# Sums over features and heads: constant-matrix products in float32r halves, and late gates' tanh at another place

## The chip, the cores and the metric

The kernel runs on one core of a Trainium2 chip. A core has a matrix engine (TensorE; PE in the profile, with PEld for its weight loads), VectorE (DVE), ScalarE (ACT), GpSimd (POOL) and a queue engine that issues most of the DMAs (SyncE; SP). Each engine works through its own list of instructions in order and waits for the others by semaphores. The metric is the device time of one execution in microseconds (us); lower is better.

## The reference

One layer of a hybrid block on x of 512 frames by 1024 features, all in float32. What matters here, shortened:

```python
def rms_norm(x, g):
    return x * lax.rsqrt(jnp.mean(x * x, axis=-1, keepdims=True) + 1e-6) * g

x = x + 0.5 * swiglu(rms_norm(x, ffn1_norm), w1, w3, w2)        # d_ff = 2816
p = rms_norm(x, mix_norm) @ W_in
# rwkv7_mixer on token-shifted columns of p, 8 heads of 64:
kk = kk / maximum(sqrt(sum(kk * kk)), 1e-12)                    # per head
y = rwkv7_recurrence(r, decay, k, v, -kk, kk * a)               # state per head, frame by frame
mu = mean(y); var = mean(square(y - mu))                        # per head
y = (y - mu) * rsqrt(var + eps) * lnx_g + lnx_b
bonus = sum(r * k * r_k) * v                                    # per head
y_a = ((y + bonus) * (sigmoid(g_lo) @ g_up)) @ rwkv_proj
y_b = forgetting_attention(rms_norm(q), rms_norm(k), v, log_f) @ fox_proj
x = x + (sigmoid(g_A) * y_a + sigmoid(g_B) * y_b) @ w_out
x = x + 0.5 * swiglu(rms_norm(x, ffn2_norm), w1, w3, w2)
out = rms_norm(x, final_norm)
```

## The kernel before, in words

Activations lie transposed: features on the 128 partitions, the 512 frames along the free dimension. x is 8 tiles of 128x512 (`xT`). A large product is made of float32r products of 128x128 weights by 128x512 activations. float32r is a float32 with a shortened mantissa, so every operand is split in two halves: `hi`, a cast to float32r (ScalarE, `act.copy`), and `lo`, the rest (VectorE, a subtraction). `mm3` (L122 to L125) then makes three products: whi by xhi, whi by xlo, wlo by xhi. A float32r product of this size shows as one record, a full float32 one as two.

Weights come as blocks of up to 8x128x128: `load_raw` (DMA, three buffers `raw`), then `split_w` (cast at L115 into one of two buffers `whi`, subtraction at L116 into one of two `wlo`). A cast into `whi` must wait until the products that read that buffer's previous content are through.

The stages, with their place in the profiled execution:

1. 0 to 26 us: x is loaded and transposed, the first gate and up column of the first FFN is made as the tiles arrive (`f0`, `f1`). `Norm.square` takes squares of the 8 tiles and adds seven of them in `acc` (GpSimd or VectorE); the eighth stays in `last`.
2. To 380 us: first FFN, 22 column pairs (`pa`, `pb`), then 8 output blocks (`pd`). `Norm.finish` (L192) sums the squares over partitions with a product by the matrix `ones`, once for `acc` (L194) and once for `last` (L195), in full float32; then ln (`rln`) and exp (`rstd`, L199) on ScalarE. The gate reads `rstd` at L329 (`fa`) and so empties the bank of `pa`.
3. 380 to 406: mixer's norm finish, the low-rank codes (`pl`, `pz`) with their sigmoids (L455).
4. 406 to 520: four steps `step(p)`, one per head pair: columns k, r, v and a gate, small products per chunk (`gp`), the key norm's head sum, and the bonus: `rk` = r k r_k, summed per head by a full float32 product with `bones`, the block matrix of ones (L589), then times v and stored.
5. 540 to 726: the delta rule as a scan over 16 chunks of 32 frames, with the attention and its columns filling between; each chunk writes its part of `V4` (the four tiles `vs`).
6. 726 to 784, the late stage: `fox_proj` (`ppj<-yh`), interleaved with the head norm of the rule: `yc` = `center` by y (L881, full float32, `center` is identity less mean), its square, the variance sum with `bones` (L885, full float32), ln, exp, scale and shift, the output gate product (L893), and the split in `ya`. Then `rwkv_proj` (`ppj<-ya`). The merge gates of the first seven columns get their tanh at L918, all behind `roots`, the last head pair's exp, since another table set has to be loaded on ScalarE for tanh.
7. To 830 `w_out` (`pw`), then second FFN and final norm to 1207.

The order on each engine is set when the kernel is built: a scheduler with its own estimate of durations lists the instructions of each engine by data dependences, free buffers and a few marks (`tc.issue_after(x)`: not before x in the list; `tc.keep_in_program_order`). On the chip each list runs strictly in order. PSUM banks come from three pools: `pm` (2 banks), `pr` (3) and `pf` (3).

The attention's q and k norms sum their squares already by two float32r products with `bonesr`, through the helper `headsum` (cast L136, subtraction L139, products L140 and L141).

Of the kernel before, what the change touches and what calls it, by code (L numbers as in the profile page):

```python
# [9 lines left out]
F32 = mybir.dt.float32  # L10
F32R = mybir.dt.float32r
BF16 = mybir.dt.bfloat16
AF = mybir.ActivationFunctionType
ALU = mybir.AluOpType
# [4 lines left out]
P = 128  # L19
T = 512  # L20
# [5 lines left out]
NP = DA // P  # L26
# [24 lines left out]
def kernel(  # L51
# [7 lines left out]
    dve, act, pool, pe = nc.vector, nc.scalar, nc.gpsimd, nc.tensor  # L59

    cp = ctx.enter_context(tc.tile_pool(name="cp", bufs=1))
# [8 lines left out]
    def bank(name, pool_=None):  # L70
        pool_ = pool_ or pm
        return pool_.tile([P, T], F32, tag="b", name=name)

    def tmp(name, shape=(P, T), dt=F32, tag="t", **kw):
        return tp.tile(list(shape), dt, tag=tag, name=name, **kw)
# [5 lines left out]
    dve.tensor_copy(identb[:], ident[:])  # L81
    ones = cp.tile([P, P], F32, name="ones")
    dve.memset(ones[:], 1.0)
    bones = cp.tile([P, P], F32, name="bones")
    dve.memset(bones[:], 0.0)
    dve.memset(bones[0:64, 0:64], 1.0)
    dve.memset(bones[64:128, 64:128], 1.0)
    center = cp.tile([P, P], F32, name="center")
    dve.scalar_tensor_tensor(center[:], bones[:], -1.0 / 64, ident[:], op0=ALU.mult, op1=ALU.add)
    bonesr = cp.tile([P, P], F32R, name="bonesr")  # L90
    dve.tensor_copy(bonesr[:], bones[:])
# [37 lines left out]
        tc.keep_in_program_order(pre)  # L129
        tc.keep_in_program_order(act.activation(out, in_, AF.Ln, **kw))  # L130

    def headsum(ps, src, hi=None, lo=None, eng=None):
        hi = tmp("shi", dt=F32R)[:] if hi is None else hi
        lo = tmp("slo", dt=F32R)[:] if lo is None else lo
        if eng is act:
            act.copy(hi, src)  # L136
        else:
            dve.tensor_copy(hi, src)
        dve.tensor_tensor(lo, src, hi.bitcast(F32), op=ALU.subtract)  # L139
        pe.matmul(ps, bonesr[:], hi, start=True, stop=False)  # L140
        pe.matmul(ps, bonesr[:], lo, start=False, stop=True)  # L141

    def split(dst_hi, dst_lo, src, hi_eng="act"):
        if hi_eng == "act":
            act.copy(dst_hi, src)
        else:
            dve.tensor_copy(dst_hi, src)
        dve.tensor_tensor(dst_lo, src, dst_hi.bitcast(F32), op=ALU.subtract)


    xctx = ExitStack()
# [3 lines left out]
    class Norm:  # L155
# [35 lines left out]

        def finish(s):  # L192
            ps = bank("ssum", pr)
            pe.matmul(ps[:], ones[:], s.acc[:], start=True, stop=False)  # L194
            pe.matmul(ps[:], ones[:], s.last[:], start=False, stop=True)  # L195
            ln = tmp("rln")
            ln_act(ln[:], ps[:], bias=epsr[:, 0:1], scale=1.0 / D)
            s.rstd = xp.tile([P, T], F32, tag="rstd", name="rstd")
            act.activation(s.rstd[:], ln[:], AF.Exp, scale=-0.5)  # L199
# [10 lines left out]
    def pc(i):  # L210
        return par[:, i:i + 1]
# [11 lines left out]
    with tc.tile_pool(name="x0", bufs=1) as x0:  # L223
# [7 lines left out]
        for c in range(KD):  # L231
            ps = bank("xtp", pr)
# [149 lines left out]
    with ExitStack() as mx:  # L382
        rp = mx.enter_context(tc.tile_pool(name="rp", bufs=1))
# [6 lines left out]
        def duo(tag, name, dt=F32):  # L390
            return sp.tile([P, 2, T], dt, name=name, tag=tag)
# [30 lines left out]
        la = rp.tile([P, T], F32, name="la", tag="la")  # L422
# [27 lines left out]
        for p in range(NP):  # L450
            za.append((zslots[2 * p], zslots[2 * p + 1]))
            for i, (w_, x_, par0, o) in enumerate(((uw, lw, PAR_W0, zslots[2 * p]), (ux, lx, PAR_A0, zslots[2 * p + 1]))):
                ps = bank("pz", (pr, pf)[i])
# [7 lines left out]
        t2 = pctx.enter_context(tc.tile_pool(name="t2", bufs=1, side="right"))  # L461
# [8 lines left out]
        vs = [V4[:, p] for p in range(NP)]  # L470
# [10 lines left out]
        def work(name, dt=F32):  # L481
            late = name in ("kka", "rk", "bon")
            return t2.tile([P, T], dt, name=name, tag="sb" if late else "sa", bufs=3 if late else 5)
# [23 lines left out]
        def step(p):  # L507
# [10 lines left out]
            sq = work("ksq")  # L518
            act.activation(sq[:], kk[:], AF.Square)
            hi, lo = work("khi", F32R), work("klo", F32R)  # L520
# [15 lines left out]
            ps = bank("pn", pf)  # L536
# [3 lines left out]
            rn = work("krn")  # L540
# [8 lines left out]
            for q in range(2):  # L549
                s = slice(q * 64, (q + 1) * 64)  # L550
                dve.scalar_tensor_tensor(G[p][q][s, :, 0, :], ch(kk)[s], -1.0, Pp[s, :, 0:C],
                                         op0=ALU.mult, op1=ALU.mult)
            for q in range(2):
                s = slice(q * 64, (q + 1) * 64)
# [6 lines left out]
            for a_ in range(2):  # L561
                with tc.issue_after(mms[5].ins):
                    for c in range(8):
                        for q in range(2):
                            g = (a_ + q) % 2
                            s = slice(q * 64, (q + 1) * 64)
# [3 lines left out]
                for q in range(2):  # L570
                    g = (a_ + q) % 2
# [5 lines left out]
                        op=ALU.mult)  # L577
# [7 lines left out]
            rk = work("rk")  # L585
            dve.scalar_tensor_tensor(rk[:], r[:], pc(PAR_RK + p), k[:], op0=ALU.mult, op1=ALU.mult)
            ps = bank("pn", pr)
            with tc.issue_after(gm.ins):
                pe.matmul(ps[:], bones[:], rk[:], start=True, stop=True)  # L589
            bon = work("bon")  # L590
            dve.tensor_tensor(bon[:], ps[:], v[:], op=ALU.mult)
            act.activation(bon[:], bon[:], AF.Identity, bias=pc(PAR_LB + p))
# [7 lines left out]
        t2 = fctx.enter_context(tc.tile_pool(name="fx", bufs=1, side="right"))  # L600
# [8 lines left out]
        for t in range(C - 1):  # L609
            n, m = t + 1, C - 1 - t  # L610
# [47 lines left out]
        def norm_qk(p):  # L658
            if p < NP // 2:
                for o, par0 in qks[p]:  # L660
                    dve.tensor_tensor(o[:], o[:], mix.rstd[:], op=ALU.mult)
            sums = []
            for o, par0 in qks[p]:
                sq = tmp("qsq")
                act.activation(sq[:], o[:], AF.Square)
                ps = bank("pq2", pf)
                headsum(ps[:], sq[:], eng=act)
                sums.append(ps)
            for (o, par0), ps in zip(qks[p], sums):
                rn = tmp("qrn")  # L670
                act.activation(rn[:], ps[:], AF.Ln, bias=epsr[:, 0:1], scale=1.0 / 64)
                qks["last"] = act.activation(rn[:], rn[:], AF.Exp, scale=-0.5)
                dve.scalar_tensor_tensor(o[:], o[:], pc(par0), rn[:], op0=ALU.mult, op1=ALU.mult)
            qks[p] = [o for o, par0 in qks[p]]
# [95 lines left out]
        dve.scalar_tensor_tensor(nf[FR, :], fz[FR, :], 0.0, nf[FR, :], op0=ALU.min, op1=ALU.subtract)  # L770
        dve.tensor_tensor_scan(fz[FR, :], ones[FR, 0:1].broadcast_to([8, T]), nf[FR, :], initial=0.0, op0=ALU.mult, op1=ALU.subtract)

        klc = [t2.tile([P, T], F32R, name=f"klc{q}") for q in range(2)]
        for q in range(2):
            o = (1 - q) * 64
            pool.memset(f32(klc[q][:]), 0.0)
# [7 lines left out]

        yb = []
        pts = t2.tile([P, 2, T], F32, tag="pt", name="pts")
        qb = [rp.tile([P, T], F32R, name="qb0", tag="la"), t2.tile([P, T], F32R, name="qb1")]
        for p in range(NP):
            qp, kp = qks[p]
            qa = [t2.tile([P, T], F32R, tag=f"qa{q}", name=f"qa{q}") for q in range(2)]  # L790
            kb = [t2.tile([P, T], F32R, tag=f"kb{q}", name=f"kb{q}") for q in range(2)]
# [13 lines left out]
            for i, bl in enumerate(((0, 1), (2,), (3,))):  # L805
# [3 lines left out]
                for q in range(2):  # L809
                    lp = pf.tile([P, T], F32, tag="b", name="lp")  # L810
                    lps.append(lp)
                    for b in bl:
                        n, bs = (b + 1) * P, slice(b * P, (b + 1) * P)
# [4 lines left out]
                for q in range(2):  # L818
                    pt, mx = pts[:, q], mx_[q]
                    for b in bl:  # L820
                        n, mb = (b + 1) * P, mx[:, b:b + 1]
# [47 lines left out]
        ya = [duo(f"BK{p}", f"ya{p}", F32R) for p in range(NP)]  # L869
        ya = [[t[:, i] for i in range(2)] for t in ya]  # L870
# [4 lines left out]
        bons = gslot[12:16]  # L875
        for p in range(NP):
            nc.sync.dma_start(bons[p], bsave[p])
        for p in range(NP):
            y = vs[p]
            yc = bank("yc", pr)  # L880
            pe.matmul(yc[:], center[:], y, start=True, stop=True)  # L881
            sq = gslot[8 + p % 2]
            act.activation(sq, yc[:], AF.Square)
            ps = bank("pg", pf)
            pe.matmul(ps[:], bones[:], sq, start=True, stop=True)  # L885
            rn = tslot[p]
            with tc.issue_after(logs.ins):
                act.activation(rn, ps[:], AF.Ln, bias=epsl[:, 0:1], scale=1.0 / 64)
                roots = act.activation(rn, rn, AF.Exp, scale=-0.5)
            dve.tensor_tensor(y, yc[:], rn, op=ALU.mult)  # L890
            dve.scalar_tensor_tensor(y, y, pc(PAR_LG + p), bons[p], op0=ALU.mult, op1=ALU.add)
            ps = bank("pg", pf)
            pe.matmul(ps[:], gup[0:96, p * P:(p + 1) * P], lg[0:96, :], start=True, stop=True)  # L893
            dve.tensor_tensor(y, y, ps[:], op=ALU.mult)
            split(*ya[p], y)

        ybs = []
        for p in range(NP):
# [4 lines left out]
        for m in range(KD):  # L903
            g = gslot[m]
            nc.gpsimd.dma_start(g, gsave[KD + m])
            ps = proj(m, fox_proj, ybs)
# [5 lines left out]
        for m in range(KD):  # L912
            nc.gpsimd.dma_start(slot[m], gsave[m])
            if NP <= m < NP + 3:
                dve.tensor_tensor(slot[m], slot[m], mix.rstd[:], op=ALU.mult)
            if m < NP + 3:
                with tc.issue_after(roots.ins):
                    act.activation(slot[m], slot[m], AF.Tanh, scale=0.5)  # L918
        rtp = ctx.enter_context(tc.tile_pool(name="xr2", bufs=1, side="right"))
        xT[:] = [rtp.tile([P, T], F32, name=f"xS{c}") for c in range(KD)]  # L920
        for c in range(KD):
            nc.gpsimd.dma_start(xT[c][:], xsave[c])
        ms = []
# [3 lines left out]
        for m in range(KD):  # L927
            g = slot[m]
            ps = proj(m, rwkv_proj, ya)
            dve.scalar_tensor_tensor(g, g, 1.0, ps[:], op0=ALU.add, op1=ALU.mult)  # L930
            dve.tensor_tensor(g, g, gslot[m], op=ALU.add)
            ms.append((mh[m], ml[m]))
            split(*ms[m], g)
        for m in range(KD):
            wh, wl = load_w([(0, w_out[0][:, m * P:(m + 1) * P])], KD, P)
            ps = bank("pw")
# [77 lines left out]
```

## Time and profile before

| | us |
|---|---|
| median of 3 runs | 1209.44 (1207.71 to 1210.8) |
| profiled execution, its own time | 1208.85 |
| its span | 1207.0 |
| TensorE busy | 1186.6 (98%) |
| VectorE busy | 653.4 (54%) |
| ScalarE busy | 449.7 (37%) |
| GpSimd busy | 102.6 (9%) |

The profile is of one execution. A group row names line, engine, operation, output and inputs, shape, the count, and after the bar the busy time, the mean duration of one in ns, and the idle time of the engine just ahead of them with what ended it. A timeline row gives start and duration in us, the same names, and in brackets the idle time ahead and its releaser. Matmuls overlap in the pipeline, so the distance between starts tells what one costs, not its duration.

### The profile page before, as it was taken

The numbers are of one execution on the slowest core, as the hardware profiler recorded it, in microseconds if no ns is written. First come the engines' busy times: TensorE is split into PE (matmuls) and PEld (weight loads), VectorE is DVE, ScalarE is ACT, GpSimd is POOL, SyncE is SP. The second block draws the span as 40 slices with busy tenths as digits, with TensorE's granted clock in tenths as the row PEclk, the third lists the DMA queues.
The fourth block names the chain that finished last, engine by engine and source line by source line (L and its number), as shares of the span: only waits on it lengthen the run. The fifth ranks groups of instructions, "written<-read, shape, count | busy, mean of one in ns | idle before, by whom it ended". The sixth has DMA issues, their size and how long they took to land. (4 is left out here: it accounts for less than half of the span.)

```text
span 1207.0 us, 15844 instructions
## 1 busy us (share of the span) xinstructions
PE 1186.6 (98%) x6340; PEld 953.7 (79%) x6340; DVE 653.4 (54%) x974; ACT 449.7 (37%) x724; POOL 102.6 (9%) x144
## 2 busy tenths in 40 slices
PE   8999999999999999999999999999999999999997
PEld 6888888888887787887767776777888888888887
DVE  6454545533443687686766655765554545543232
ACT  6222222212223754346876755423222222222221
POOL 4200000001111112401000011111000000000110
PEclk9999999999999999999999999999999999999999
DMA  6333333323333333344112135633333333323331
GB/s 183 101 88 105 88 105 90 102 84 109 112 113 93 103 109 115 103 137 114 54 45 86 54 98 163 192 105 88 101 91 101 92 105 88 105 80 95 96 96 71
DMA packets 208153, 122.54 MB, mean 102 GB/s; under 512 B 9903, under 2 KB 200431, under 8 KB 208079
## 3 DMA queue, kind: packets, MB, share of 16 engines
q1 hardware_dynamic: 202078, 108.67, 30.8%
q0 software_dynamic: 3760, 12.06, 3.1%
q8 instruction: 50, 0.82, 0.3%
q10 hardware_dynamic: 2240, 0.79, 0.3%
q14 instruction: 25, 0.20, 0.1%
HBM read 110.82 MB, written 10.68 MB: 101 GB/s over the span
## 5 line engine op out<-in xcount | busy, mean ns | idle before, releaser
L115 ACT CAST whi<-raw 128x1024 fp32r<-128x1024 f32 (+3 forms) x199 | 198.4, 998 | 633.6 <-PE pa L124 178.8
L116 DVE TENSOR_TENSOR wlo<-raw,whi 128x1024 fp32r<-128x1024 f32 (+2 forms) x198 | 229.2, 1158 | 132.5 <-ACT whi L115 130.5
L123 PE MATMUL pa<-xh,whi 128*128 128x512 f32 x344 | 134.6, 391 | 0.0
L125 PE MATMUL pb<-xh,wlo 128*128 128x512 f32 x344 | 133.9, 389 | 0.6 <-DVE wlo L116 0.6
L123 PE MATMUL pb<-xh,whi 128*128 128x512 f32 x344 | 134.2, 390 | 0.0
L125 PE MATMUL pa<-xh,wlo 128*128 128x512 f32 x344 | 133.9, 389 | 0.0
L124 PE MATMUL pa<-xl,whi 128*128 128x512 f32 x344 | 133.8, 389 | 0.0
L124 PE MATMUL pb<-xl,whi 128*128 128x512 f32 x344 | 133.8, 389 | 0.0
L125 PE MATMUL pd<-hh,wlo 128*128 128x512 f32 x330 | 131.2, 398 | 0.0
L123 PE MATMUL pd<-hh,whi 128*128 128x512 f32 x330 | 130.3, 395 | 0.0
L124 PE MATMUL pd<-hl,whi 128*128 128x512 f32 x330 | 130.3, 395 | 0.0
L333 DVE TENSOR_TENSOR fb<-pb,rstd 128x512 f32<-128x512 f32 x43 | 29.7, 691 | 137.2 <-PE pb L125 137.2
L125 PEld LDWEIGHTS pb<-xh,wlo 128*128 128x128 f32 x344 | 64.6, 188 | 14.5 <-DVE wlo L116 1.0
L123 PEld LDWEIGHTS pa<-xh,whi 128*128 128x128 f32 x344 | 64.6, 188 | 13.8 <-issue 0.5
L124 PEld LDWEIGHTS pb<-xl,whi 128*128 128x128 f32 x344 | 64.6, 188 | 13.7 <-issue 0.2
L124 PEld LDWEIGHTS pa<-xl,whi 128*128 128x128 f32 x344 | 64.5, 188 | 13.6 <-issue 0.2
L123 PEld LDWEIGHTS pb<-xh,whi 128*128 128x128 f32 x344 | 64.5, 188 | 13.6 <-ACT whi L115 0.2
L125 PEld LDWEIGHTS pa<-xh,wlo 128*128 128x128 f32 x344 | 64.5, 188 | 13.4
L124 PEld LDWEIGHTS pd<-hl,whi 128*128 128x128 f32 x330 | 62.0, 188 | 14.9
L125 PEld LDWEIGHTS pd<-hh,wlo 128*128 128x128 f32 x330 | 62.0, 188 | 14.8 <-issue 0.2
L123 PEld LDWEIGHTS pd<-hh,whi 128*128 128x128 f32 x330 | 62.0, 188 | 14.8 <-issue 0.2
L329 DVE TENSOR_TENSOR fa<-pa,rstd 128x512 f32<-128x512 f32 x43 | 29.7, 691 | 73.2 <-PE pa L125 72.9
(367 smaller groups left out, 1954.8 us busy)
## 6 DMA issues: line engine op xcount, KB each, us to landing
raw<-in_ffn_w_dram SPq DMA_DIRECT2D x118, 512.0 KB
raw<-in_w_in_dram SPq DMA_DIRECT2D x40, 512.0 KB
raw<-in_ffn_w_dram SPq DMA_DIRECT2D x15, 384.0 KB
raw<-in_w_out_dram SPq DMA_DIRECT2D x8, 512.0 KB
gsave<-gs SPq DMA_DIRECT2D x9, 256.0 KB
xin<-in_x_dram SPq DMA_DIRECT2D x4, 512.0 KB
xsave<-xT POOLq DMA_DIRECT2D x8, 256.0 KB, 2.3
G<-gsave POOLq DMA_DIRECT2D x8, 256.0 KB, 3.6
```

Source lines behind the costliest of these rows:

```text
L115: act.copy(hi[:], raw[:])
L116: (eng or dve).tensor_tensor(lo[:], raw[:], hi[:].bitcast(F32), op=ALU.subtract)
L123: pe.matmul(ps, whi, xhi, start=first, stop=False)
L124: pe.matmul(ps, whi, xlo, start=False, stop=False)
L125: return pe.matmul(ps, wlo, xhi, start=False, stop=last)
L329: dve.tensor_tensor(a[:], pa[:], nrm.rstd[:], op=ALU.mult)
L333: dve.tensor_tensor(b[:], pb[:], nrm.rstd[:], op=ALU.mult)
```

## The change

It has five parts.

- `ones` gets a float32r copy `onesr`; `center` becomes float32r; `bones` remains only as a source for `bonesr` (and `center`).
- `headsum` becomes `exact(ps, mat, src)`: cast of the source on ScalarE, subtraction on VectorE, two float32r products with a given constant matrix. The matrices hold only 0, 1, -1/64 and 63/64.
- `Norm.finish` adds `last` to `acc` on VectorE and takes one `exact` with `onesr` in place of two float32 products.
- In `step`, `rk` is split and summed by two float32r products with `bonesr`. In the late stage the four tiles `vs` are split first, into buffers that the attention has left (`parts`), `yc` is two float32r products with `center`, and the variance sum is `exact` with `bonesr`.
- The tanh of the late gates: three stand behind the cast of the last `ya`, and each further one behind the cast of the merged column three before it, instead of all seven behind `roots`.

Products with `gup` (L893) and those of the final norm stay in float32.

```diff
+    onesr = cp.tile([P, P], F32R, name="onesr")
+    dve.tensor_copy(onesr[:], ones[:])
...
-    center = cp.tile([P, P], F32, name="center")
+    center = cp.tile([P, P], F32R, name="center")
...
+    def exact(ps, mat, src):
+        hi, lo = tmp("shi", dt=F32R), tmp("slo", dt=F32R)
+        act.copy(hi[:], src)
+        dve.tensor_tensor(lo[:], src, hi[:].bitcast(F32), op=ALU.subtract)
+        pe.matmul(ps, mat[:], hi[:], start=True, stop=False)
+        pe.matmul(ps, mat[:], lo[:], start=False, stop=True)
...
     def split(dst_hi, dst_lo, src, hi_eng="act"):
+        cast = act.copy(dst_hi, src) if hi_eng == "act" else dve.tensor_copy(dst_hi, src)
         dve.tensor_tensor(dst_lo, src, dst_hi.bitcast(F32), op=ALU.subtract)
+        return cast
...
         def finish(s):
             ps = bank("ssum", pr)
-            pe.matmul(ps[:], ones[:], s.acc[:], start=True, stop=False)
-            pe.matmul(ps[:], ones[:], s.last[:], start=False, stop=True)
+            dve.tensor_tensor(s.acc[:], s.acc[:], s.last[:], op=ALU.add)
+            exact(ps[:], onesr, s.acc[:])
...
             ps = bank("pn", pr)
+            hi, lo = work("rhi", F32R), work("rlo", F32R)
+            split(hi[:], lo[:], rk[:])
             with tc.issue_after(gm.ins):
-                pe.matmul(ps[:], bones[:], rk[:], start=True, stop=True)
+                pe.matmul(ps[:], bonesr[:], hi[:], start=True, stop=False)
+                pe.matmul(ps[:], bonesr[:], lo[:], start=False, stop=True)
...
+        parts = [[t2.tile([P, T], F32R, tag=f"{n}{q}", name=f"y{n}{q}")[:] for q in range(2)] for n in ("qa", "kb", "klc")]
+        parts.append([rp.tile([P, T], F32R, tag="la", name="yla")[:], t2.tile([P, T], F32R, tag="qb1", name="yqb")[:]])
+        for p in range(NP):
+            split(*parts[p], vs[p])
...
-            pe.matmul(yc[:], center[:], y, start=True, stop=True)
+            for i in range(2):
+                pe.matmul(yc[:], center[:], parts[p][i], start=i == 0, stop=i == 1)
...
-            pe.matmul(ps[:], bones[:], sq, start=True, stop=True)
+            exact(ps[:], bonesr, sq)
...
-                roots = act.activation(rn, rn, AF.Exp, scale=-0.5)
+                act.activation(rn, rn, AF.Exp, scale=-0.5)
...
-            split(*ya[p], y)
+            parted = split(*ya[p], y)
...
+        def late_tanh(m, behind):
             if m < NP + 3:
-                with tc.issue_after(roots.ins):
+                with tc.issue_after(behind.ins):
                     act.activation(slot[m], slot[m], AF.Tanh, scale=0.5)
+
+        for m in range(3):
+            late_tanh(m, parted)
...
-            split(*ms[m], g)
+            late_tanh(m + 3, split(*ms[m], g))
```

More of the change, by code (lines that the diff above doesn't have):

```diff
@@ L83 @@
     dve.memset(ones[:], 1.0)
-    bones = cp.tile([P, P], F32, name="bones")
+    onesr = cp.tile([P, P], F32R, name="onesr")
+    dve.tensor_copy(onesr[:], ones[:])
+    bones = tmp("bones", (P, P))
     dve.memset(bones[:], 0.0)
@@ L130, in ln_act @@
         tc.keep_in_program_order(act.activation(out, in_, AF.Ln, **kw))
[L132 to L141, printed above, removed]
+    def exact(ps, mat, src):
[4 more added lines that the diff above has]
+        pe.matmul(ps, mat[:], lo[:], start=False, stop=True)
     def split(dst_hi, dst_lo, src, hi_eng="act"):
[L144 to L147, printed above, removed]
+        cast = act.copy(dst_hi, src) if hi_eng == "act" else dve.tensor_copy(dst_hi, src)
         dve.tensor_tensor(dst_lo, src, dst_hi.bitcast(F32), op=ALU.subtract)
+        return cast
     xctx = ExitStack()
@@ L666, in norm_qk @@
                 ps = bank("pq2", pf)
-                headsum(ps[:], sq[:], eng=act)
+                exact(ps[:], bonesr, sq[:])
                 sums.append(ps)
@@ L771 @@
         dve.tensor_tensor_scan(fz[FR, :], ones[FR, 0:1].broadcast_to([8, T]), nf[FR, :], initial=0.0, op0=ALU.mult, op1=ALU.subtract)
-        klc = [t2.tile([P, T], F32R, name=f"klc{q}") for q in range(2)]
+        klc = [t2.tile([P, T], F32R, name=f"klc{q}", tag=f"klc{q}") for q in range(2)]
         for q in range(2):
@@ L786 @@
         pts = t2.tile([P, 2, T], F32, tag="pt", name="pts")
-        qb = [rp.tile([P, T], F32R, name="qb0", tag="la"), t2.tile([P, T], F32R, name="qb1")]
+        qb = [rp.tile([P, T], F32R, name="qb0", tag="la"), t2.tile([P, T], F32R, name="qb1", tag="qb1")]
         for p in range(NP):
```

## The prediction

> **What bounds the kernel.** I read the page first, then the groups of instructions with shapes kept apart, then the timeline around every place that the diff touches. The page:
>
> ```profile
> span 1207.0 us, 15844 instructions
> PE 1186.6 (98%) x6340; PEld 953.7 (79%) x6340; DVE 653.4 (54%) x974; ACT 449.7 (37%) x724; POOL 102.6 (9%) x144
> PEclk9999999999999999999999999999999999999999
> PE 36%; DVE 0%; ACT 0%; issue 0%; DVEq 0%
> ```
>
> TensorE is busy for 98% of the span at its full clock, and the chain that ended last names it alone. So work taken from TensorE shortens the span, unless TensorE then waits in its place; work given to VectorE (54%) and ScalarE (37%) is free, unless TensorE waits for it. Each edit is therefore judged twice: products saved, and what TensorE's next instruction waits for.
>
> **The price of a product.** The groups that go, then their start times in the timeline (start, duration, engine, line):
>
> ```profile
> L194 PE MATMUL ssum<-acc,ones 128*128 128x512 f32 x6 | 3.1, 604 | 0.1
> L195 PE MATMUL ssum<-sq,ones 128*128 128x512 f32 x6 | 3.1, 592 | 0.0
> L589 PE MATMUL pn<-rk,bones 128*128 128x512 f32 x8 | 4.5, 644 | 0.0
> L881 PE MATMUL yc<-V,center 128*128 128x512 f32 x8 | 3.8, 592 | 0.0
> L885 PE MATMUL pg<-G,bones 128*128 128x512 f32 x8 | 4.1, 591 | 0.0
> ```
> ```profile
> 835.56 1.02 PE L194 MATMUL ssum<-acc,ones 128*128 128x512 f32 x2
> 836.64 0.40 PE L125 MATMUL pb<-xh,wlo 128*128 128x512 f32 x1
> 836.88 0.39 PE L123 MATMUL pb<-xh,whi 128*128 128x512 f32 x1
> 837.11 0.39 PE L124 MATMUL pb<-xl,whi 128*128 128x512 f32 x1
> ```
>
> A float32 product shows as two records, so x6 is three products. Durations overlap; starts tell the cost. float32r products follow each other at 0.23 us (836.64, 836.88, 837.11). From 835.56 to 836.64 lie one float32 and one float32r product: 1.08 - 0.23 = 0.85 us for the float32 one. Two float32r in its place take 0.45, so each exchange saves 0.40 us. A norm's finish has two float32 products and gets one pair: 1.70 - 0.45 = 1.25 us.
>
> **The nominal gain** is 3 x 1.25 + 12 x 0.40 (4 bonus sums, 4 centrings, 4 variance sums) = 8.6 us. In exchange ScalarE gets 15 casts and VectorE 15 subtractions and 3 additions, at the rates of the groups that do this for the attention's norms already: cast 0.62, subtraction 0.69 (below), so 9.3 and 12.4 us. Whether they are hidden depends on the place.
>
> ```profile
> L136 ACT CAST shi<-qsq 128x512 fp32r<-128x512 f32 x8 | 4.9, 618 | 1.7 <-issue 1.6
> L139 DVE TENSOR_TENSOR slo<-qsq,shi 128x512 fp32r<-128x512 f32 x8 | 5.5, 690 | 4.3 <-PE pq L140 3.0 <-ACT shi L136 1.1
> ```
>
> **1. First FFN's norm: a loss of 3.3 us.** Its rows:
>
> ```profile
> 24.90 1.10 PE L194 MATMUL ssum<-acc,ones 128*128 128x512 f32 x2
> 25.83 1.02 PE L195 MATMUL ssum<-sq,ones 128*128 128x512 f32 x2
> 27.92 0.50 PE L125 MATMUL pb<-xh,wlo 128*128 128x512 f32 x1 [0.60 <-DVE wlo L116]
> 33.03 0.39 PE L123 MATMUL pa<-xh,whi 128*128 128x512 f32 x1
> ```
> ```profile
> 24.01 1.99 ACT L115 CAST whi<-raw 128x1024 fp32r<-128x1024 f32 x2
> 26.89 0.69 ACT L130 ACTIVATE rln<-ssum,epsr 128x512 f32<-128x512 f32 x1 [0.89 <-PE ssum L195]
> 27.61 0.63 ACT L199 ACTIVATE rstd<-rln 128x512 f32<-128x512 f32 x1
> 33.00 1.05 ACT L115 CAST whi<-raw 128x1024 fp32r<-128x1024 f32 x1 [2.81 <-PE pb L124]
> ```
> ```profile
> 25.09 2.77 DVE L116 TENSOR_TENSOR wlo<-raw,whi 128x1024 fp32r<-128x1024 f32 x2 [0.34 <-ACT whi L115]
> 28.28 0.69 DVE L329 TENSOR_TENSOR fa<-f,rstd 128x512 f32<-128x512 f32 x1 [0.41 <-ACT rstd L199]
> ```
>
> Before the change both sums run ahead of pb, so rstd and fa (which empties the bank that pa needs) are done at 28.97, four microseconds before pa at 33.03. In the changed order the sum of the upper half comes before pb, but that of the lower half only after 23 of pb's 24 products. ScalarE's order is then: two weight casts, the cast of the sum, table load, the weight cast that waits for the end of pb's products (33.00 above), and only behind it the logarithm. Queued behind that cast wait the logarithm, rstd and the gates' table load; behind the next wlo on VectorE waits fa. The chain: the upper cast cannot start before 26.0 (end of the two weight casts), so TensorE idles until 26.6, as long as the old sums took, and the saved 1.25 us are gone. The addition ahead of wlo on VectorE moves pb's third product from 27.92 to some 28.2 and pb's end from 33.0 to 33.3. The weight cast runs 33.3 to 34.3, then logarithm to fa's end, 28.97 - 26.89 = 2.08 us: pa starts at about 36.4, not 33.03. TensorE has one or two products meanwhile. Net +3.3 us; +2.0 if the weight cast slips behind the logarithm, +3.6 at most.
>
> The trace has TensorE slow after a wait, at the beginning:
>
> ```profile
> 11.60 0.63 PE L123 MATMUL f<-xh,whi 128*128 128x512 f32 x1
> 12.02 0.63 PE L124 MATMUL f<-xl,whi 128*128 128x512 f32 x1
> ```
>
> Products start 0.43 us apart there, half rate. [...]
>
> **2. Mixer's norm: -0.4 us.** Two products fewer give -1.25. But rstd now comes through addition, cast, subtraction and a later sum. The last two code products and the first product of the first step are where before waited:
>
> ```profile
> 401.79 2.42 ACT L455 ACTIVATE G<-pz,par 128x512 f32<-128x512 f32 x4 [2.61 <-PE pz L454]
> 405.69 1.29 DVE L489 TENSOR_TENSOR u<-pk,rstd 128x512 f32<-128x512 f32 x2 [5.25 <-PE pz L454]
> 406.43 0.50 PE L123 MATMUL pk<-xh,whi 128*128 128x512 f32 x1 [0.78 <-DVE u L489]
> ```
>
> In the new order a weight cast (1.05 us, behind the first step's last product with the old weights) stands ahead of the code sigmoids (2.42 / 4 = 0.60 each), and the last two code products wait for the first two sigmoids. On a clock of before, moved by the 0.85 us of the sum that ran during the down projection, the cast goes from 403.4 to 404.5, the sigmoids to 405.7, the last code product to 406.2 and u (0.69) to 406.9, where 406.43 stood: +0.5 - 0.85 = -0.35. Behind the cast wait the remaining sigmoids and the table load of the steps, 2.4 us later than before; the second step's weights (its cast is in the same queue) still come 1 us early. Ends: -1.25 (no sigmoid late) and +1.0 (both sigmoids late by another cast).
>
> **3. Four steps: -1.6 us.** The bonus sum's halves come from work slots, the product stands behind the chunk products, and its reader (bonus times v, then a store) feeds nothing of TensorE's. In the window 406 to 520 TensorE waits 0.8 us in all, the one row above. ScalarE is busy there for half of the time, so cast and subtraction fit. Without that cover each step costs 0.62 + 0.69.
>
> **4. Scan: 0.** The order on TensorE is the same; 0.5 us either way.
>
> **5. Late stage: -2.3 us.** Eight exchanges give -3.1 (from the second of these rows to the third are 34 products, 0.233 apart, so 0.39 each). And the wait moves:
>
> ```profile
> 725.98 0.50 PE L123 MATMUL ppj<-yh,whi 128*128 128x512 f32 x1 [0.20 <-DVE gs L633]
> ...
> 775.71 0.39 PE L124 MATMUL ppj<-ya,whi 128*128 128x512 f32 x1
> ...
> 783.64 0.39 PE L125 MATMUL ppj<-ya,wlo 128*128 128x512 f32 x1
> ```
>
> ```profile
> 752.06 0.63 ACT L889 ACTIVATE Tall<-Tall 128x512 f32<-128x512 f32 x1
> 752.71 1.28 ACT L918 ACT_TABLE_LOAD   x1
> 754.01 3.75 ACT L918 ACTIVATE ga<-ga 128x512 f32<-128x512 f32 x7
> 757.67 0.60 ACT L115 CAST whi<-raw 128x512 fp32r<-128x512 f32 x1
> ```
> ```profile
> 755.73 0.40 PE L125 MATMUL ppj<-yh,wlo 128*128 128x512 f32 x1
> 758.32 0.50 PE L123 MATMUL ppj<-yh,whi 128*128 128x512 f32 x1 [2.19 <-ACT whi L115]
> ```
>
> Before the change a weight cast queued behind table load and seven tanh holds TensorE for 758.32 - 755.73 - 0.23 = 2.36 us. That goes. What is late next is ya3, the rule's last operand. From the first late product on (725.98), 113 float32r and 4 float32 products bring the last variance sum to 725.98 + 26.4 + 3.4 = 755.8. Then Ln, Exp, three VectorE operations, cast and subtraction, at about 0.7 us a link (2.08 for the three links from 26.89 to 28.97) and 0.4 for the product's own end, are through at 761.3; TensorE has 17 products (4.0 us) meanwhile and waits 0.9 + 0.3 us. Behind ya3's cast (760.6) ScalarE loads the table (1.28), does three tanh (0.54 each) and only then the next weight cast, until 764.1: TensorE has run out at 762.3 and waits 1.9, then 0.1 for the next. New waits 3.2 against 2.36, net -3.1 + 0.8 = -2.3. Ends: -5.5 if none of the new waits arises, +0.9 if they are twice as long.
>
> The row says that a table load costs ScalarE 754.01 - 752.71 = 1.30 us. [...]
>
> **6. Second FFN's norm: -1.25 us.** 48 products of the first two columns stand ahead of the sum, so addition, cast and subtraction (2 us) run under them, and the next banks are needed 48 products (11 us) after it. If the logarithm stood on the path as in 1, this would be +2.
>
> No DMA of the large loads moves: on SP one gate's store goes behind one weight load of the late stage and one bonus store a place ahead; both have readers many microseconds later, so I cost it at nothing (what hides it is that distance; a late store would hold a tanh, 0.54).
>
> **Sum.** 3.3 - 0.4 - 1.6 + 0 - 2.3 - 1.25 = -2.25 us of 8.6 nominal. The profiled run took 1208.85 us (span 1207.0 and 1.85 around it): 1206.6. It lies 0.6 below the median of 1209.44, which gives 1207.2; I say 1207. That is 0.2% under the median, less than the 0.3% (3.6 us) that a measurement of this kernel tells from no change.
>
> **Rivals.**
> *Nominal gain arrives (faster).* Late waits do not arise and the first norm's logarithm gets past the weight cast: -5.5 in place of -2.3 alone gives 1204; both, 1202.5. For it: ScalarE is idle for 2.8 us ahead of 33.00. Against: each engine works in its order, and that order puts the cast first.
> *The steps become bound by VectorE (slower).* Grouping by stage:
>
> ```profile
> 406.00:520.00 114.00, 113.57 (x703) 91.40 (x704) 90.67 (x125) 55.13 (x76) 26.88 (x49) 1.00 0.38 110
> ```
>
> Columns are TensorE, weight loads, VectorE, ScalarE, GpSimd. VectorE is 80% busy here, the highest anywhere. If its order delays a wlo or a u in each step by cast and subtraction (1.31), four steps give +5.2 instead of -1.6: 1207 + 6.8 = 1214. It decides once the delay passes 0.4 + 1.2 us a step. Against: only 0.8 us of waits now.
> *Clock halved after the long wait at 36.* Ten products at 0.43 instead of 0.23 would add 2, so 1209, no change. For it: the slow products above. Against: none show behind the wait of 2.36 us in the late stage, beyond the first three products. [...]
> *Nothing gained:* waits at all places take what the products give, 1209, no change.
>
> **Chances.** Forecast 0.42, nothing gained 0.06, clock 0.04, nominal gain 0.30, steps bound (or another place with its price) 0.18. The first three are within 0.3%, less 0.02 for forecasts that end beyond it: same 0.50, faster 0.32, slower 0.18. The forecast's own range is 1204.5 to 1209.5; with the ends of 2 and 5 and the rivals' nearer parts 1203 to 1212.
>
> **What would show it.** In the changed profile: a wait of some 3 us at the first pa after pb (about 33 to 36.4), released by fa; two sigmoid waits near 405; no new wait between 406 and 520; the wait at 755.7 gone, and one of about 2 us at the third rwkv_proj column, released by a weight cast or tanh, after about 1 us for ya; no wait behind the second FFN's sum. TensorE's busy time down by some 8 us. I am wrong if ScalarE takes the logarithm first, if the late chain is shorter, or if a step waits.

## The result, and the profile after

The changed kernel is slower: 1211.99 us in the median (1209.12 to 1214.59, 20 runs) against 1209.83 (1207.57 to 1211.86, 20 runs), ratio 1.0017 with a 95% interval of 1.0010 to 1.0023. The forecast was 0.2% faster, so the sign was wrong; the size, +0.17%, is within the 0.3% that the prediction called no change. The profiled execution took 1211.94 us, its span 1210.2, that is 3.2 us more than the span before.

The page after:

```profile
span 1210.2 us, 15874 instructions
PE 1184.5 (98%) x6334; PEld 955.1 (79%) x6334; DVE 665.2 (55%) x993; ACT 458.1 (38%) x739; POOL 100.5 (8%) x144
PEclk9999999999999999999999999999999999999999
core 0: 1210.2 us, clock 0.992
```

TensorE's busy time fell by 2.1 us only, where the exchanged products should take 8 off. The mean granted clock is 0.992; it was 0.996. Over the 20 runs the same shows: the six at a clock of 0.994 took 1209.1 to 1210.3 us, the twelve at 0.992 or less 1211.5 to 1214.6. The row of clock digits shows nothing of it, since each digit is a mean over 30 us. The timeline after, around the first norm (start, duration, engine, line):

```profile
34.21 0.40 PE L127 MATMUL pb<-xh,wlo 128*128 128x512 f32 x1
37.25 0.50 PE L125 MATMUL pa<-xh,whi 128*128 128x512 f32 x1 [2.64 <-DVE fa L326]
37.58 0.40 PE L126 MATMUL pa<-xl,whi 128*128 128x512 f32 x1
37.82 0.42 PE L127 MATMUL pa<-xh,wlo 128*128 128x512 f32 x1
38.05 0.61 PE L125 MATMUL pa<-xh,whi 128*128 128x512 f32 x1
38.46 0.63 PE L126 MATMUL pa<-xl,whi 128*128 128x512 f32 x1
...
41.02 0.60 PE L126 MATMUL pa<-xl,whi 128*128 128x512 f32 x1
41.45 0.41 PE L127 MATMUL pa<-xh,wlo 128*128 128x512 f32 x1
41.70 0.40 PE L125 MATMUL pa<-xh,whi 128*128 128x512 f32 x1
```

The forecast wait is there: pa starts at 37.25, released by fa. But 0.8 us behind it products start 0.43 us apart instead of 0.23, for 3.4 us (38.05 to 41.45): eight products that each cost 0.2 us more, 1.6 us. Stretches of the same kernel (columns: stretch, its length, TensorE busy and instructions, granted clock, DMA share, GB/s):

```profile
27.60:31.40 3.80, 3.80 (x10) 0.55 0.86 255
31.40:37.20 5.80, 3.20 (x15) 1.00 0.01 4
38.00:41.60 3.60, 3.60 (x10) 0.53 0.45 133
```
```profile
409.00:412.60 3.60, 1.95 (x7) 1.00 0.36 101
413.50:417.00 3.50, 3.50 (x10) 0.51 0.29 87
```
```profile
625.00:629.00 4.00, 2.05 (x18) 0.95 0.00 0
629.00:631.50 2.50, 2.50 (x6) 0.50 0.00 0
```

Four times TensorE's granted clock falls to 0.50, each time for 3.413 us: behind the waits for the first norm's upper sum and for pb's weights (from 27.82), behind the wait for fa (38.06), behind the mixer's norm (413.52), and in the scan (628.56). The profile of before has no such stretch between its loading phase and the end; behind its own waits at these places it reads:

```profile
28.50:34.00 5.50, 5.50 (x26) 1.00 0.50 149
407.00:412.00 5.00, 5.00 (x23) 1.00 0.38 105
622.50:626.00 3.50, 3.50 (x36) 1.00 0.00 0
```

Its loading phase does have one (clock 0.50 from 10.36 to 13.78, the rows at 11.60 in the prediction), and that of the changed kernel's profile has none.

Between landmarks of TensorE (first instruction of each kind), after less before, and the forecast:

| stretch | measured | of it half rate | rest | forecast |
|---|---|---|---|---|
| start to first `pd` (first norm) | +5.96 | 3.3 | +2.7 | +3.3 |
| `pd` to first `pgt` (mixer's norm, codes) | +1.73 | 1.6 | +0.1 | -0.4 |
| `pgt` to first `xps` (four steps) | -1.64 | 0 | -1.6 | -1.6 |
| `xps` to first `ppj` (scan) | +1.08 | 1.0 | +0.1 | 0 |
| `ppj` to first `pw` (late stage) | -2.67 | 0 | -2.7 | -2.3 |
| `pw` to the end (second norm) | -1.26 | 0 | -1.3 | -1.25 |
| sum | +3.20 | 5.9 | -2.7 | -2.25 |

Half rate is counted as products at 0.43 us times 0.2 us: 8 + 8 and the edges, 8, and 5. This split is an estimate from one pair of profiles. The first row holds a piece of luck from the loading phase, which the change does not touch: with a slow stretch there, the kernel before starts its last product of `f` at 24.39 us; without one, the changed kernel does so at 23.53. Counted from there, the rest of the first norm is 3.5 us and not 2.7.

### The profile page after: what moved, and what is told of

It reads as the page before. It is cut to its first block, busy times and chain, and to the rows that moved or that the text cites. A ratio compares the mean times of both kernels' runs of the same rounds, so it can differ in the third digit from the quotient of the medians.

```text
span 1210.2 us, 15874 instructions
## 1 busy us (share of the span) xinstructions
PE 1184.5 (98%) x6334; PEld 955.1 (79%) x6334; DVE 665.2 (55%) x993; ACT 458.1 (38%) x739; POOL 100.5 (8%) x144
## 4 chain that ended last, share of the span: by engine, by line
PE 93%; DVE 3%; ACT 1%; issue 0%; DMA 0%; DVEq 0%; POOL 0%; POOLq 0%
PE pd L127 7%; PE pd L125 7%; PE pd L126 7%; PE pa L125 7%; PE pa L126 7%; PE pa L127 6%; PE pb L127 6%; PE pb L126 6%; PE pb L125 6%; PE pgt L125 3%; PE pgt L127 2%; PE pgt L126 2%; PE pk L125 2%; PE pk L127 2%; PE pk L126 2%; PE pw L127 1%
```

## The experiments

Two theories are tested. **H**: TensorE gets half its clock for about 3.4 us when it was mostly idle over a stretch of that length, and those stretches are cut by a clock of their own (the 3.4 is the length of the slow stretches in the two profiles so far), so that the same wait brings it in one execution and not in the next. **C**: the slow products come from something at those places in the kernel, such as weight loads and casts (the DMA share was 0.86 in the first of them).

**The changed kernel again** (no edit).

> The changed kernel itself, profiled a second time. Theory H (TensorE is run at half rate for about 3.4 us after a stretch of that length in which it was mostly idle, the stretches being cut by a clock that runs free of the kernel): again two to four stretches of products 0.43 us apart, 3.4 us long each, but not necessarily at the same places, and starting at multiples of 3.41 us from each other; profiled time between 1207 and 1215 accordingly. Rival C (products are slowed where they collide with weight loads or casts): the same places as in the first profile (27.8, 38.1, 413.5, 628.7) and nowhere else. Ratio to before 1.002 in both.

1211.67 us (11 runs), ratio 1.0017 (1.0006 to 1.0028). Its profile:

```profile
22.00:33.00 11.00, 8.22 (x35) 1.00 0.33 96
33.00:36.90 3.90, 0.71 (x3) 1.00 0.00 0
36.90:40.40 3.50, 3.50 (x10) 0.52 0.51 150
409.00:412.40 3.40, 1.75 (x5) 0.99 0.25 52
412.40:415.90 3.50, 3.50 (x10) 0.52 0.42 123
```

Two more lie in the scan (627.4) and in the loading phase (9.6). So three of the four stretches of the first profile came again, and the one at 28 did not, with the same order and the same waits ahead of it. That speaks for H. And the distances fit a period of 3.413 us, the length of one slow stretch: in the first profile 38.06 - 27.82 = 10.24, 3 times that, and 413.52 - 38.06 = 375.5, 110 times; in the second, by the first slow products, 412.48 - 36.98 = 375.5.

Two distances alone would fit other periods nearly as well. The granted clock of the profiles settles it. In the first profile of the changed kernel half rate starts at 27.82, 38.06, 413.52, 628.56 and, close to the end, 1205.42 us: the distances from the first are 3, 113, 176 and 345 times 3.4133 us. In that of the kernel before it starts at 10.36 and 1201.61, 349 times 3.4133 us apart. The 14 profiles of this document hold 49 such starts, and every distance from the first of a profile is a whole multiple of 3.4133 us, to within 0.02 us. Cut each profile on this grid, and H can be read off directly. Between 20 and 1185 us, of the stretches that TensorE began at full clock, every one in which it was busy for 0.48 of the time or less is followed by half rate, and none in which it was busy for more than 0.63; in between either happens. (In the first profile of the changed kernel and that of before, the stretches followed by half rate were 0.24, 0.38, 0.43 and 0.59 busy, and the least busy of the others 0.49, 0.54 and 0.65.) The waits at 28 show why the first profile pays for them and the second does not. In the first (first line) both waits fall into one stretch, 0.38 busy; in the second (other two lines) they fall into two:

```profile
24.40:27.82 3.42, 1.29 (x4) 1.00 0.13 37
```
```profile
23.22:26.64 3.42, 1.72 (x8) 1.00 0.00 0
26.64:30.05 3.41, 2.33 (x10) 1.00 0.61 176
```

The price can be read off in the same way, from stages with the same code that are followed by half rate in one profile and not in another:

| stage | with half rate | without |
|---|---|---|
| `pd` to first `pgt`, mixer's norm as changed | 157.54 to 157.55 (4 profiles) | 155.91 (1, the filled kernel below) |
| `xps` to first `ppj` (scan) | 166.3 to 166.8 (8) | 164.9 to 165.4 (6) |
| late stage as changed | 56.73, 56.75 (2) | 55.21 to 55.26 (4) |
| late stage as before | 59.18 to 59.35 (3) | 57.90 (1) |

**Filling the first norm's waits.**

`fill(n, x)` puts n products of `onesr` by the first tile's upper half behind x, into a bank that nobody reads: 8 behind the last product of `f`, 12 behind pb's last.

```diff
+        fill(8, fmm)
...
+                    if j == 1 and first:
+                        fill(12, cm[-1])
```

> The changed kernel with 8 products by onesr of no use ahead of the first norm's upper sum and 12 behind pb's last product, ahead of pa. They fill TensorE's two waits there and leave its inputs and the length of the waits alone. Theory H: no stretch at half rate at 27.8 and at 38.1; pa still starts 3 to 4 us later than before the change, minus the first stretch (1.6), so at 35.6; time 3.3 us below the changed kernel, ratio to before 0.9995. Rival C: both slow stretches stay and the ratio stays at 1.002.

1209.17 us (12 runs), ratio 0.9992 (0.9983 to 1.0001). The profile of the filled kernel:

```profile
32.51 2.97 PE L247 MATMUL dummy<-xh,onesr 128*128 128x512 f32 x12
35.89 0.50 PE L125 MATMUL pa<-xh,whi 128*128 128x512 f32 x1 [0.41 <-DVE fa L336]
36.23 0.39 PE L126 MATMUL pa<-xl,whi 128*128 128x512 f32 x1
```
```profile
27.60:31.40 3.80, 3.80 (x19) 1.00 0.80 232
36.00:40.00 4.00, 4.00 (x18) 1.00 0.45 131
```

pa still waits for fa, 3.6 us behind the start of pb's last product (32.28 to 35.89). Both slow stretches are gone while the DMA share in them is as high as before (0.80, 0.45). C falls. More work on TensorE made the kernel 2.5 us faster than the changed one (1211.67 in the same series), where H had forecast 3.3. This profile has half rate in one place only, the scan; its span is 1205.5 us, 1.5 less than that of before, in spite of 20 useless products. (The fill also moved some instructions of the four steps; their stretch got shorter by 0.1 us only. That no half rate follows the mixer's norm here is the place of the grid, not the fill: TensorE was 0.72 busy in the stretch ahead.)

**First two norms as before, the rest changed.**

```diff
-            dve.tensor_tensor(s.acc[:], s.acc[:], s.last[:], op=ALU.add)
-            exact(ps[:], onesr, s.acc[:])
+            if s.gain != PAR_FFN2:
+                pe.matmul(ps[:], ones[:], s.acc[:], start=True, stop=False)
+                pe.matmul(ps[:], ones[:], s.last[:], start=False, stop=True)
+            else:
+                dve.tensor_tensor(s.acc[:], s.acc[:], s.last[:], op=ALU.add)
+                exact(ps[:], onesr, s.acc[:])
```

> The changed kernel, but the first FFN's and the mixer's norm finish as before, by two float32 products each; the second FFN's norm, the four steps, the late stage as changed. If the loss is in the waits of these two norms and the half rate behind them: -1.25 (second FFN) - 1.6 (steps) - 2.7 (late stage) = -5.5 us against before, 1204.3, ratio 0.9955, and no slow stretch near 28, 38 and 413. Rival: the new waits of the late stage or the steps also cost, then no more than -2 us, ratio 0.998.

1204.83 us (5 runs), ratio 0.9961 (0.9947 to 0.9974): -4.5 us, near the -5.5 forecast. The loss sat in the first two norms. Its profile shows where the missing microsecond can come from: half rate behind the late stage's new wait, which the profile of the changed kernel happened not to have.

```profile
762.08 0.70 PE L125 MATMUL ppj<-ya,whi 128*128 128x512 f32 x1 [1.57 <-ACT whi L117]
```
```profile
756.00:762.50 6.50, 4.27 (x16) 0.98 0.98 352
762.50:766.00 3.50, 3.50 (x10) 0.56 0.47 139
```

**Only one of the two norms as before.** The same edit with `s.gain == PAR_FFN1`, then with `s.gain == PAR_MIX`, in place of `s.gain != PAR_FFN2`.

> The changed kernel, only the first FFN's norm finished as before (two float32 products). Theory H with waits: the loss of the first norm (some 5 to 6 us in the two profiles of the changed kernel up to the first pd) goes, the mixer's stays (0.1 us of waits beyond its saved products, and 1.6 when the half rate follows): 1206, ratio 0.997. Rival M (the mixer's norm loses as much as the first): 1208 to 1209, ratio 0.999.

> The changed kernel, only the mixer's norm finished as before. H with waits: the first norm's loss stays, 1210, ratio 1.0005. Rival M: 1208, ratio 0.999.

With the first FFN's norm as before: 1204.8 us (6 runs), 0.9962 (0.9947 to 0.9977), not to be told from the kernel with both as before. With the mixer's norm as before: 1210.73 (12 runs), 1.0008 (0.9999 to 1.0017). So M falls and the first FFN's norm carries the loss: the last kernel and the one with both as before (1204.83) differ by this norm alone, and by 5.9 us. In the profiles, too, all kernels with the old first norm on an otherwise untouched first stage reach the first `pd` at 255.1 to 257.1 us, those with the new one, unfilled, at 261.5 to 264.3. What the mixer's exchange is worth, the medians do not settle: nothing by one pair (0.9962 and 0.9961), 1.1 us by the other (1.0017 and 1.0008), with intervals that overlap. Its stage takes 157.55 us where half rate follows (four of five profiles) and 155.91 where it does not, against 155.81 in the kernel before: it saves nothing, and costs 1.7 us where the half rate comes.

**Only the late tanh moved, on the kernel before.** The diff's `late_tanh`, with `parted` the last cast of `ya`, and nothing else.

> The kernel before with only the late tanh moved (three behind the last ya cast, the others behind the casts of the merged columns). TensorE's order is that of before. If the wait of 2.36 us at 755.7 is only moved behind ya3: a wait of about 2 us at the third rwkv_proj column in its place, ratio 0.9995 to 1.000. If most of it goes: -2 us, ratio 0.9985.

1206.49 us (11 runs), 0.9977 (0.9968 to 0.9986). That is more than the -2 of the better forecast. The profiled execution is the slowest of the eleven (1209.55), with half rate in the scan. In it a wait of 1.2 us at the third rwkv_proj column replaces that of 2.36. From 725.98 to the first `pw` the kernel before took 57.90 us, this one 56.71: 1.2 us, while the runs show 2.8. In the three kernels under "A wait alone" below, whose late stage is that of before, half rate follows the same wait in all three profiles; in that of before the wait fell into a stretch (754.46 to 757.87) that was 0.49 busy, and none followed. So part of the executions of before seem to pay for it, too, and not the one profiled. That remainder is argued, not shown.

**First two norms as before, and the late tanh as before.**

```diff
-                act.activation(rn, rn, AF.Exp, scale=-0.5)
+                roots = act.activation(rn, rn, AF.Exp, scale=-0.5)
...
-        for m in range(3):
-            late_tanh(m, parted)
+        for m in range(KD):
+            late_tanh(m, roots)
...
-            late_tanh(m + 3, split(*ms[m], g))
+            split(*ms[m], g)
```

> The kernel with the first two norms as before and the rest changed (1204.8), but the late gates' tanh all behind the last head pair's exp, as before the change. If the place of the tanh is what made the late stage shorter: ya3's cast waits behind table load and seven tanh (5 us), TensorE waits some 2 to 3 us more in front of ya3's products, less the wait of 2 us for the third column that goes: +1 to +2.5, 1206 to 1207.3, ratio 0.9975. If the exchanged products alone carry the late stage's gain: no difference, 0.996.

1206.49 us (12 runs), 0.9975 (0.9966 to 0.9983): 1.7 us worse than with the tanh moved, as forecast; but the intervals overlap (0.9947 to 0.9974 there), so this run alone does not settle what the move is worth on the changed kernel. In the two profiles, both with half rate in the late stage, it takes 57.58 and 56.75 us. In the profile of this run TensorE waits for ya3's cast, which stands behind table load and tanh:

```profile
761.25 0.73 PE L125 MATMUL ppj<-ya,whi 128*128 128x512 f32 x2 [3.27 <-ACT ya L143]
```

**Filling the late wait as well.** The kernel with the first two norms as before, and (`proj.last` is the last product of the column before):

```diff
             ps = proj(m, rwkv_proj, ya)
+            if m == 1:
+                dummy = bank("dummy", pf)
+                with tc.issue_after(proj.last.ins):
+                    for _ in range(8):
+                        pe.matmul(dummy[:], onesr[:], ya[0][0], start=True, stop=True)
```

> The kernel with the first two norms as before and the rest changed, and 8 products of no use in TensorE's wait ahead of the third rwkv_proj column. The profile without them (1204.8 median) had seven products at half rate just behind that wait. Theory H: no half rate there, 0.7 us lower in the median (it does not come in every run) and a narrower spread; ratio 0.9955. Rival C: the half rate stays. Third: the useless products hold back the third column, +0.5.

1204.13 us (6 runs), 0.9955 (0.9941 to 0.9968), and in its profile full rate behind the filled wait:

```profile
752.00:761.50 9.50, 8.84 (x36) 1.00 0.90 279
761.50:766.00 4.50, 4.50 (x21) 1.00 0.62 202
```

The difference to the kernel without the fill, 0.7 us, is as forecast but within the intervals. The same fill with only the first norm as before:

> The changed kernel with the first FFN's norm as before, and 8 products of no use in the wait ahead of the third rwkv_proj column. Candidate: from 1204.8 (ratio 0.9962) some 0.7 lower if the half rate behind that wait goes: ratio 0.9956, as the one that has the mixer's norm as before too (0.9955). If the mixer's waits cost half rate in most runs, the other one is better by up to 1.

1205.06 us (5 runs), 0.9957 (0.9943 to 0.9970): the four best kernels (0.9955 to 0.9962) cannot be told apart. All are faster than both kernels of this case.

**A wait alone.** On the kernel before, copies of the first norm's logarithm onto itself make `rstd` late; every product and its order stay.

```diff
+            if s.gain == PAR_FFN1:
+                for _ in range(8):
+                    act.copy(ln[:], ln[:])
```

The second kernel has 10 copies. The third has 10 copies and 14 useless products behind pb's last.

> The kernel before with 8 copies of the first FFN's logarithm onto itself on ScalarE, ahead of rstd. Every product is the same and in the same order; the copies use up the 4.06 us that fa was early by, so that TensorE waits some 2.4 us at the first pa (about 33.0 to 35.4). Theory H: the half rate follows when most of one stretch of 3.41 us falls in the wait, so in a part of the runs: +2.4 to +4.0, middle +3.2, ratio 1.0026. Theory W (a wait costs its own length): +2.4, ratio 1.0020.

> As before, with 10 copies: a wait of 3.7 us. Theory H: some stretch of 3.41 us is always mostly idle, so always half rate for about 3.4 us behind it: +3.7 + 1.6 = +5.3, ratio 1.0044, and products 0.43 us apart behind the wait in the profile. Theory W: +3.7, ratio 1.0031. [...]

> 10 copies, and 14 products of no use by bonesr behind pb's last product, which fill 3.2 of the 3.7 us. pa starts when it does without them. Theory H: no half rate, +3.7, ratio 1.0031, 1.6 us less than without the useless products. Theory W: as without them.

The first pa in the kernel with 8 and in that with 10 copies:

```profile
36.22 0.80 PE L123 MATMUL pa<-xh,whi 128*128 128x512 f32 x1 [3.06 <-DVE fa L332]
```
```profile
35.54 0.50 PE L123 MATMUL pa<-xh,whi 128*128 128x512 f32 x1 [3.70 <-DVE fa L332]
```

| kernel | wait at pa (starts less 0.23) | median | ratio (interval) | more than before |
|---|---|---|---|---|
| 8 copies | 3.2 | 1215.94 | 1.0044 (1.0031 to 1.0056) | 6.0 |
| 10 copies | 3.9 | 1217.06 | 1.0055 (1.0043 to 1.0068) | 7.1 |
| 10 copies, filled | filled | 1213.90 | 1.0029 (1.0017 to 1.0040) | 3.9 |

The wait of 8 copies came out at 3.2 us instead of 2.4 (the next weight cast stands between the last copy and `rstd`). Theory W, that a wait costs its own length, would give 3.2, 3.9 and 3.9; it fits only the filled kernel. The clock behind the same wait, unfilled and filled:

```profile
37.00:41.00 4.00, 4.00 (x12) 0.60 0.29 88
```
```profile
37.00:41.00 4.00, 3.82 (x17) 1.00 0.44 129
```

So useless products in a wait of 3.9 us give back 3.2 us in the medians, twice what H had forecast. The profiles show 1.6 of it: from the first `pa` to the first `pd` 224.9 us unfilled, 223.3 filled. A further 1.4 us between the two profiles lies in the scan (166.4 and 164.9 us), which the fill does not touch: there half rate follows in the unfilled one only. In the profile of 8 copies two stretches of half rate follow each other, 35.4 to 42.3, and products are slow from 36.81 to 41.93; no other profile has that between the loading phase and the end. The profiles account for 1.7 us (10 copies) and 2.7 us (8 copies) of half rate at this place. With the wait that makes 5.9 of the 6.0 us for 8 copies, and 5.6 of the 7.1 for 10; the rest stays open.

## Why the prediction was wrong

**The step that failed** is the weighing of the rival "Clock halved after the long wait at 36": 0.04, one place, +2 us, so "no change", and no term of the sum. The runs show half rate at up to four places, 5.9 us together in the profile, and without it, by the table above, the kernel would have come out 2.7 us faster (1.8 without the luck in the loading phase), near the -2.25 forecast. The filled kernel, which has the same waits and no half rate behind the first norm's two, is 2.5 us faster than the changed one. One stretch was priced at ten products, 2 us, by an estimate; it measured eight, 1.6 us. The argument against the rival was that none shows behind the wait of 2.36 us in the late stage. One profile of one wait was taken as a rule, though the same wait brings half rate in other executions. And the waits that the change adds were counted as their own length only.

No single gap as long as a slow stretch (3.413 us) was needed: a gap of 2.8 us (34.4 to 37.25) was enough in the first profile of the changed kernel, one of 3.35 us (33.25 to 36.60) in the second, and in both so were the mixer's three waits of 1.0, 0.35 and 1.05 us within 3 us of each other. In the first profile the stretch of the grid that holds these three (410.11 to 413.52) was 0.59 busy.

**Step by step.**

- *Price of a product, nominal gain*: right. The four steps and the second norm, where nothing waits, gave -1.64 and -1.26 against -1.6 and -1.25.
- *1, first norm*: the mechanism is right, cast before logarithm, fa as releaser, and so is its size: a rest of +2.7 to +3.5 against +3.3. ScalarE's rows after show the order:

```profile
34.17 1.05 ACT L117 CAST whi<-raw 128x1024 fp32r<-128x1024 f32 x1 [7.31 <-PE pb L126]
35.13 0.68 ACT L132 ACTIVATE rln<-ssum,epsr 128x512 f32<-128x512 f32 x1
35.84 0.63 ACT L196 ACTIVATE rstd<-rln 128x512 f32<-128x512 f32 x1
```

- *1, half rate*: it added 3.3 us to this, at two places (from 27.82 and from 38.06), where the sum had no term for it.
- *2, mixer's norm*: the two sigmoid waits and that for u came (410.67, 411.24, 412.52); 0.5 us more than forecast, and 1.6 us of half rate behind them. The medians of the single-norm kernels do not settle what is left of it.
- *4, scan*: order and waits unchanged, as said; that half rate can follow the scan's own waits was missed. It does so in the profiles of several kernels, not in that of before.
- *5, late stage*: right. Waits of 0.8, 0.2 and 1.7 us where 1.2 and 2.0 were forecast:

```profile
767.77 0.73 PE L125 MATMUL ppj<-ya,whi 128*128 128x512 f32 x2 [0.66 <-ACT ya L143]
771.26 0.51 PE L125 MATMUL ppj<-ya,whi 128*128 128x512 f32 x1 [1.56 <-ACT whi L117]
```

- The table load ahead of the tanh took 1.30 us again (767.73 to 769.03), and the tanh starts at its end, with no gap, as in the trace of before (752.71 to 754.01):

```profile
767.73 1.28 ACT L925 ACT_TABLE_LOAD   x1
769.03 1.67 ACT L925 ACTIVATE ga<-ga 128x512 f32<-128x512 f32 x3
```

- *The slower rival*, steps bound by VectorE, did not occur.

## What to carry to other kernels

In these runs a new wait of TensorE cost its length and, where a stretch of the 3.413-us grid was busy for 0.48 or less (in some profiles up to 0.63), some 1.6 us of half rate behind it (2.7 where two slow stretches followed each other). Where the grid lay differed from execution to execution (the first slow product behind the wait for fa started at 38.05 us in one profile of the changed kernel and at 36.98 in the other), so the same wait cost this in one and not in the next, as the one at 28 did. A sum that stays within the measurement's limit without this term can change its sign with it. Look for it in windows of 3 to 4 us behind each wait, since the page's clock digits average it away, and take more than one profile before saying that a wait does not bring it. Before a product is made cheaper, see whether it stood in a place where TensorE would have waited anyway (as the old sums of the first norm did); there the costlier form is the better one, and where a wait must stay, products that nobody reads can fill it: in the filled kernel the granted clock stayed at 1.00 from 22 to 40 us, in the changed one it was 0.55 and 0.53 in the two slow stretches.

## What was not expected of the hardware

Useless products made the kernel faster: 20 of them in the first norm 2.5 us, 14 behind an artificial wait 3.2 us. The starts of slow stretches within one execution lie at multiples of 3.413 us from each other, over the whole 1200 us (from 27.82 to 1205.42 in the first profile of the changed kernel, 345 times), and differ in place between two executions of the same kernel. The 20 runs of the changed kernel spread over 5.5 us and those of before over 4.3. Each run's granted clock shows where this comes from: in the 29 runs of before that stand beside the first experiments, the ten at a clock of 0.997 or more took 1207.4 to 1209.4 us, the thirteen at 0.995 or less 1209.2 to 1211.8. The spread follows the time at half rate; that the waits are its only source is not shown.
